# Attention by query pair first: out projection, LN1 and routing moved into the attention loop of a hybrid decoder layer

## The chip, the cores and the metric

One core of one Trainium2 chip runs the whole program. The metric is the device time of one execution, in microseconds (us). The kernel before takes 1218.9 us (median of three runs, 1218.84 to 1220.23). The profile is one further execution.

## The reference, cut to what matters

The layer takes 1024 tokens of width 1024, puts 16 meta tokens in front, and normalises them. A token mixer follows with two head groups, then one output projection, a residual and a layer norm (LN1), then a mixture of experts. Cut to what the change touches:

```python
# stick-breaking attention: 8 heads x 64, strictly causal, blocks of 128 queries
z = q @ k.T * scale
log_not_beta = where(visible, -softplus(z), 0)
between = reverse_cumsum(log_not_beta) - log_not_beta
o_sb = rms_norm(where(visible, exp(log_sigmoid(z) + between), 0) @ v, sb_norm_g)
# gated DeltaNet: 4 heads x 128, a recurrence over chunks of the sequence -> o_gdn
h = layer_norm(ALPHA * h + concat([o_sb, o_gdn]) @ w_out, ln1_g, ln1_b)    # out projection, LN1
group = top1(h @ w_group + b_group); experts = top2(expert logits in that group)   # routing
y[token] = sum over its 2 experts of SwiGLU(h[token])                     # 32 experts
out = layer_norm(ALPHA * h + y, ln2_g, ln2_b)[meta tokens dropped]
```

A query row needs all 8 heads of the attention before its out projection, and all tokens need their routing before the first expert can gather its rows, because a token's place in an expert's list is a running count over all tokens.

## The kernel before, in words

**Stages.** `phase1` normalises, projects q, k, v and the DeltaNet inputs and prepares the recurrence. `phase2` holds the attention, the recurrence, the out projection, LN1 and the routing. `phase4` runs the 32 experts and the last norm. Instructions are put in order by a planner, which walks through the program with simulated times and may start later work early where its inputs and buffers are there; attention steps have a raised priority (`high_priority`, L1332 and L1342). Inside `manual_schedule` the order is that of the program. Each engine and the DMA queue of SP then run their instructions in that order and wait where an input is missing.

**Attention.** A unit is a head h and a pair u of 128-query tiles (tiles 2u and 2u+1). It goes through four parts one loop step apart: `at_a` (L846: scores z on PE, two sigmoids on ACT, four causal masks on POOL), `at_b` (L874: two reverse scans and one product on DVE), `at_c` (L887: transposes on PE, copies on ACT) and `at_d` (L909: product with v on PE). A pair sees 416, 928, 1440 and 1952 score columns for u = 0, 1, 2, 3. `at_e` (L928) normalises the outputs that share a PSUM bank. The units (L1307) go head by head over u = 0, 1, 2 (24 units), then u = 3 for the 8 heads. For u below 3, `at_e` takes the three pairs of a head and writes them to DRAM (`mixa`, L924). `load_h` (L804) brings q and k of a head for 768 queries or for the last 256.

**What runs between.** `gseq` (L1042) is the recurrence, four parts for a tile (`g1` to `g4`); `mid1` (L1361) takes three steps of it in each of the first three loop steps, then one. `wo_load` and `wo_split` (L951, L957) bring the out projection's weights and split them in high and low parts, one of 16 pieces for each loop step, through one staging buffer. `hgen` (L1139) does the DeltaNet half of the out projection of all 8 tiles (`mix_split`, `omm`: 24 matmuls of 512 columns for a tile) and stores the sum in `hscr`. From loop step 27 `p3gen` (L1311) does the attention half of tiles 0 to 5, LN1 (`s1`), router logits (`s2`) and the choice of experts (`choose`).

**The tail.** After the loop the string `SEQ3` (L45) orders what is left: places of tiles 0 to 3 (`place`), the choices of tiles 4 and 5, the attention half, LN1 and router of tiles 6 and 7, their choices (7 alone as the last), the loads of 11 expert weight blocks of 1 MB (`load_raw`) and the splits of the first expert's weights (`split_k`, its subtractions on POOL by `SPK`). Then come `index` and the first expert's gather (`phase4`).

Of the kernel before, what the change touches and what calls it, by code (L numbers as in the profile page):

```python
# [8 lines left out]
F32 = mybir.dt.float32  # L9
# [10 lines left out]
KT = 8  # L20
# [11 lines left out]
U1 = 24  # L32
# [7 lines left out]
PX, CH_ = 6, 4  # L40
H0, HG_, GS = 10, (1, 2), (3, 1)
XB2, MH = 2, 2
RX = 1
SPH = (0, 2, 4, 6, 6, 8, 8)
SEQ3 = "A1 L4 b04 B1 L4 H5 A9 a46 L3 G3 b46 H6 p0 G9 B9 a67 p1 |0 O2 O1 H7 O9 p2 R3 b68 p5"  # L45
XN = 3
YB = 2
SPK = (0, 1, 2, 3, 4, 5, 6, 7)
SPK1 = ()
NAT = (6, 7)  # L50
HB, WS = 3, 2
PGN = (1, 1, 1, 3, 3, 3, 3, 3, 3, 3, 3)
TB2 = 2
TG, Z1 = 2, 512
Q1 = 6 * P
G2 = 3
# [10 lines left out]
LH = ((), (0, 1))  # L67
# [12 lines left out]
class Trunk:  # L80
# [39 lines left out]
    def consts(self):  # L120
# [19 lines left out]
        self.mixa = [dram.tile([Q1, n], F32, name=f"mixa{i}") for i, n in enumerate((384, 128))]  # L140
# [280 lines left out]
    def phase1b(self, es, ps):  # L421
# [192 lines left out]
        for s, (k, i) in enumerate(jobs + [("", 0)] * 2):  # L614
            for c, _ in enumerate(cv0(s, i) if k == "g" else qk(s, i) if k == "q" else range(3)):
                step[0] = s
                if s > HG:
                    for _ in range(CA if s <= 2 * HG else CB):
                        next(inv, None)
                if c == 0:  # L620
                    if s - 1 in conv:
                        cv1(conv[s - 1])
                        cv2(conv[s - 1])
            if s == 3 * HG + 3:
                self.aqk = self.stack_v.enter_context(self.pool("aqk", "left"))
                self.qk = {}
                self.load_h(0, 0, Q1)
# [176 lines left out]
    def load_h(self, h, q0, nq):  # L804
        nc = self.nc
        nk = NM + q0 + nq
        qk = self.aqk.tile([P, Q1 + 2 * (NM + Q1)], F32R, name="qk", bufs=2)
        qs, kh, kl = qk[:, :nq], qk[:, nq:nq + nk], qk[:, nq + nk:nq + 2 * nk]
        for s in range(2):
            hs = slice(s * DH, (s + 1) * DH)  # L810
            nc.sync.dma_start(qs[hs].bitcast(F32), self.qkd[h, s, 0:DH, NM + q0:NM + q0 + nq])
# [4 lines left out]
        self.qk[h, q0] = (qs, kh, kl)  # L816
        return last

    def phase2(self):
# [20 lines left out]
        qk, st, pvs = self.qk, {}, {}  # L840
# [5 lines left out]
        def at_a(h, u):  # L846
            q0 = 0 if 2 * u * P < Q1 else Q1
            qs, kh, kl = qk[h, q0]
# [5 lines left out]
            for c0 in range((N - 1) // zc * zc, -1, -zc):  # L854
                c1 = min(N, c0 + zc)
                z = ps.tile([P, zc], F32, name="z", bufs=2)
                for i in (1, 0):
                    b0 = ns[0] * i
                    q = qs[:, (2 * u + i) * P - q0:(2 * u + i + 1) * P - q0]
# [49 lines left out]
        def at_d(h, u):  # L909
            j = u if u < 3 else h % 4  # L910
# [10 lines left out]
            if u < 3 and j == 2:  # L921
                at_e(3)
                m, c = (0, h * DH) if h < 6 else (1, (h - 6) * DH)
                nc.sync.dma_start(self.mixa[m].rearrange("(t p) c -> p t c", p=P)[:, :, c:c + DH], st["mo"])  # L924
            elif j == 3:
                at_e(4, h // 4)

        def at_e(n, g=None):  # L928
            os_ = ap.tile([P, 4, P], F32, name="os")
            nc.scalar.activation(os_[:, :n], pvs[0][:, :n], AF.Copy)  # L930
            tp = ps.tile([P, 4, P], F32, name="tp", bufs=TBC[0])
            for u in range(n):
                nc.tensor.transpose(tp[:, u], os_[:, u], self.ident)
            tv = tp[:, :n].rearrange("p u (i d) -> p (u i) d", d=DH)
            sq = ap.tile([P, 4, P], F32, name="os").rearrange("p u (i d) -> p (u i) d", d=DH)[:, :2 * n]
            nc.scalar.activation(sq, tv, AF.Square)
            rs = small.tile([P, NT], F32, name="ars")[:, :2 * n]
            nc.vector.tensor_reduce(rs, sq, axis=AX, op=ALU.add)
            self.rsqrt_into(rs, rs, 1.0 / DH, RMS_EPS)
            nc.vector.tensor_tensor(sq, tv, rs[:, :, None].to_broadcast([P, 2 * n, DH]), op=ALU.mult)  # L940
            if g is None:
                nc.gpsimd.tensor_tensor(sq, sq, gs[:, None, :].to_broadcast([P, 2 * n, DH]), op=ALU.mult)
                st["mo"] = sq
                return
            for i in range(2):
                eng = nc.gpsimd if i else nc.vector
                eng.tensor_tensor(O["ms"][i][:, g * 256:(g + 1) * 256].rearrange("p (h d) -> p h d", d=DH),
                                  sq.rearrange("p (h i) d -> p h i d", i=2)[:, :, i],
                                  gs[:, None, :].to_broadcast([P, 4, DH]), op=ALU.mult)
# [18 lines left out]
        def g_load(t):  # L968
# [12 lines left out]
            c["zg"] = gp.tile([P, 512], F32, name="zg", bufs=2)  # L981
# [93 lines left out]
        def open_out():  # L1075
            op = O["op"] = os_.enter_context(self.pool("outp", "right"))
            O["ms"] = [op.tile([P, 512], F32, name=f"ms{i}") for i in range(2)]
# [42 lines left out]
        def mix_split(t, mx):  # L1120
            m = [hp.tile([P, 4, P], F32R, name=f"m{x}", bufs=MH) for x in "hl"]
            tp = ps.tile([P, 4, P], F32, name=TQ[0], bufs=TQ[1])
            for j in range(4):
                nc.tensor.transpose(tp[:, j], mx[:, j * P:(j + 1) * P], self.ident)
            self.split(tp, *m)
            T[t]["m"] = m

        def omm(t, s, k0, al):
            ht, (mh, ml) = T[t]["ht"], T[t]["m"]
            o = ps.tile([P, 4, P], F32, name=TQ[2], bufs=TQ[3]).rearrange("p a b -> p (a b)")  # L1130
            ns = slice(s * F, (s + 1) * F)
            for j in range(4):
                wh, wl = wo[k0 + j, s]
                nc.tensor.matmul(o, mh[:, j], wh, start=(j == 0), stop=False)
                nc.tensor.matmul(o, mh[:, j], wl, start=False, stop=False)
                nc.tensor.matmul(o, ml[:, j], wh, start=False, stop=(j == 3))
            nc.vector.scalar_tensor_tensor(ht[:, ns], ht[:, ns], al, o, op0=ALU.mult, op1=ALU.add)

        def hgen():  # L1139
            while gdone[0] < 1:  # L1140
                yield
            mix_load(0)
            ht_load(0)
            for t in range(NT):
                mix_split(t, T[t]["mg"])
                yield
                omm(t, 0, 4, ALPHA)
                if t + 1 < NT:
                    while gdone[0] < t + 2:
                        yield  # L1150
                    mix_load(t + 1)
                    ht_load(t + 1)
                yield
                omm(t, 1, 4, ALPHA)
                nc.sync.dma_start(self.hscr[t * P:(t + 1) * P, :], T[t]["ht"])
                yield

        def s0(t):
            ht_load(t)
            if t < 6:  # L1160
                ma = O["op"].tile([P, 512], F32, name="mxa", bufs=1)
                nc.sync.dma_start(ma[:, :384], self.mixa[0][t * P:(t + 1) * P, :])
                nc.sync.dma_start(ma[:, 384:], self.mixa[1][t * P:(t + 1) * P, :])
            else:
                ma = O["ms"][t - 6]
            yield
            mix_split(t, ma)

        def s1(t):
            c = T[t]  # L1170
            ht = c["ht"]
            for s in range(2):
                omm(t, s, 0, 1.0)
                yield
            if t < 6:
                rs = self.ln_stats(ht, P)
                self.ln_apply(ht, P, rs, ht)
                for v, w in ((O["g1"], ALU.mult), (O["b1"], ALU.add)):
                    nc.vector.tensor_tensor(ht, ht, v, op=w)
            else:  # L1180
                c["st"] = mv, rs = self.ln_stats(ht, P, raw=True)
                yield
                nc.vector.scalar_tensor_tensor(rs[:, 1:2], mv[:, 0:1], -1.0, rs[:, 0:1], op0=ALU.mult, op1=ALU.mult)
                self.ln_apply(ht, P, rs, ht)
                for v, w in ((O["g1"], ALU.mult), (O["b1"], ALU.add)):
                    for h in range(2):
                        (nc.gpsimd if h in LH[t - 6] else nc.vector).tensor_tensor(
# [643 lines left out]
```

## Time and profile before

| | before |
|---|---|
| median of 3 runs | 1218.9 us |
| the profiled execution | 1214.15 us |
| its span, first to last instruction | 1212.3 us |
| PE busy in the span | 1087.4 us (90%) |
| DVE busy | 867.2 us (72%) |
| ACT busy | 624.9 us (52%) |
| POOL busy | 375.2 us (31%) |
| DMA | 259.20 MB, mean 214 GB/s |

PE is the matrix engine (TensorE), PEld its weight loads, DVE the vector engine, ACT the scalar engine, POOL is GpSimd, SP issues most DMAs. A busy share is an average over stages; what holds a stage is read from that stage. A name like `tp<-ident,be` is output from inputs; L899 is line 899 of the kernel. The granted clock of PE is given as a share of 2.4 GHz.

### The profile page before, as it was taken

The page shows a single profiled execution, that of the slowest core. Times are in us where ns is not written, and L with a number is a line of the kernel's source. Part 1 is how long each engine was busy: PE and PEld are TensorE (multiplying, and loading weights), DVE is VectorE, ACT ScalarE, POOL GpSimd, SP SyncE. Part 2 cuts the span into 40 slices and gives each one's busy share as a digit, 9 for nine tenths or more (in the row PEclk, how much of TensorE's full clock was granted, in tenths as well). Part 3 has the DMA queues.
Part 4 walks back from the last instruction along what each step waited for, and adds up shares of the span by engine and source line. Part 5 has one row for each costly group of instructions (what it writes and reads, how often), then busy time and mean ns, then how long its engine had stood idle before and what let it go on. Part 6 is the DMA issues. An engine that isn't in the chain of part 4 may idle for free. (4 is left out here: it accounts for less than half of the span.)

```text
span 1212.3 us, 19733 instructions
## 1 busy us (share of the span) xinstructions
PE 1087.4 (90%) x7029; PEld 925.1 (76%) x7029; DVE 867.2 (72%) x1588; ACT 624.9 (52%) x1310; POOL 375.2 (31%) x423
## 2 busy tenths in 40 slices
PE   6999999999899989789999999839999899989981
PEld 4999999999899868678777778736776666666661
DVE  7941357889433258888857687877997787887978
ACT  3443346845233244555546453326776566666754
POOL 3523103502000037666624341141222122122325
PEclk9999999999999978999989999958999999999996
DMA  7411124465896478765657672957999999998353
GB/s 284 174 62 44 54 88 124 149 199 177 249 269 206 156 243 234 220 211 152 187 158 192 209 235 101 405 219 238 343 348 333 310 324 324 325 321 270 80 197 139
DMA packets 111285, 259.20 MB, mean 214 GB/s; under 512 B 32804, under 2 KB 62252, under 8 KB 98386
## 3 DMA queue, kind: packets, MB, share of 16 engines
q1 hardware_dynamic: 101680, 239.57, 58.8%
q0 software_dynamic: 9216, 17.28, 6.1%
q8 instruction: 56, 0.92, 0.3%
q10 hardware_dynamic: 290, 1.07, 0.2%
q14 instruction: 43, 0.35, 0.1%
HBM read 205.44 MB, written 68.72 MB: 226 GB/s over the span
## 5 line engine op out<-in xcount | busy, mean ns | idle before, releaser
L184 PE MATMUL pj<-hTh,wfh 128*128 128x346 f32 (+1 forms) x480 | 156.0, 325 | 0.1
L186 PE MATMUL pj<-hTh,wfl 128*128 128x346 f32 (+1 forms) x480 | 155.6, 324 | 0.0
L185 PE MATMUL pj<-hTl,wfh 128*128 128x346 f32 (+1 forms) x480 | 155.6, 324 | 0.0
L1570 POOL DMA_INDIRECT res<-y,ix x30 | 53.4, 1780 | 233.6 <-DVE y L1566 167.1
L879 DVE TENSOR_TENSOR_SCAN mm<-mm,zero 128x272 f32<-128x272 f32 (+3 forms) x64 | 96.1, 1522 | 28.7 <-ACT mm L866 26.1
L184 PEld LDWEIGHTS pj<-hTh,wfh 128*128 128x128 f32 x480 | 90.8, 189 | 0.5 <-issue 0.3
L186 PEld LDWEIGHTS pj<-hTh,wfl 128*128 128x128 f32 x480 | 90.8, 189 | 0.1
L185 PEld LDWEIGHTS pj<-hTl,wfh 128*128 128x128 f32 x480 | 90.7, 189 | 0.2
L1461 DVE TENSOR_TENSOR w13l<-raw,w13h 128x512 fp32r<-128x512 f32 x144 | 88.9, 686 | 0.0
L1529 PE MATMUL ph<-w13h,xh 128*128 128x512 f32 x192 | 88.8, 463 | 0.0
L177 PE MATMUL pj<-wvh,hTl 128*128 128x256 f32 (+3 forms) x280 | 79.1, 286 | 3.6 <-DVE hTl L95 3.6
L176 PE MATMUL pj<-wvl,hTh 128*128 128x256 f32 (+3 forms) x280 | 79.2, 285 | 2.2 <-DVE wvl L95 2.2
L175 PE MATMUL pj<-wvh,hTh 128*128 128x256 f32 (+3 forms) x280 | 79.6, 288 | 0.3 <-ACT hTh L94 0.3
L1460 ACT ACTIVATE w13h<-raw 128x512 fp32r<-128x512 f32 x144 | 77.8, 624 | 0.0
L1531 PE MATMUL ph<-w13h,xl 128*128 128x512 f32 x192 | 75.3, 392 | 0.0
L1530 PE MATMUL ph<-w13l,xh 128*128 128x512 f32 x192 | 75.2, 391 | 0.0
L866 ACT ACTIVATE mm<-z 128x512 f32<-128x512 f32 (+1 forms) x80 | 44.1, 565 | 49.3 <-PE z L864 35.0
L870 POOL TENSOR_SCALAR_AFFINE_SELECT mm<-mm 128x128 f32<-128x128 f32 x64 | 38.6, 613 | 91.9 <-ACT mm L866 91.4
L864 PE MATMUL z<-qk 128*128 128x416 f32 (+6 forms) x224 | 61.9, 382 | 5.4 <-ACT kuw L776 3.6
L94 ACT ACTIVATE xh<-tp 128x512 fp32r<-128x512 f32 x64 | 31.4, 490 | 59.4 <-DVE xf L1516 52.9
L1461 DVE TENSOR_TENSOR w2l<-raw,w2h 128x512 fp32r<-128x512 f32 x96 | 60.0, 688 | 2.1
L870 POOL TENSOR_SCALAR_AFFINE_SELECT be<-be 128x128 f32<-128x128 f32 x64 | 47.4, 750 | 27.3 <-ACT be L867 23.0
(432 smaller groups left out, 2984.7 us busy)
## 6 DMA issues: line engine op xcount, KB each, us to landing
raw<-in_w SPq DMA_DIRECT2D x72, 1024.0 KB, 19.8
qk<-qkd SPq DMA_DIRECT2D x16, 520.0 KB, 5.3
ht<-hscr SPq DMA_DIRECT2D x16, 512.0 KB, 5.2
qk<-qkd SPq DMA_DIRECT2D x16, 392.0 KB, 6.8
kqvd<-y SPq DMA_DIRECT2D x12, 520.0 KB, 2.9
wfr<-in_w_gdn SPq DMA_DIRECT2D x12, 512.0 KB, 3.5
wo4h<-in_w SPq DMA_DIRECT2D x6, 1024.0 KB, 19.8
wo4l<-in_w SPq DMA_DIRECT2D x6, 1024.0 KB, 13.7
```

The costliest lines, as they stand in the source:

```text
L175: nc.tensor.matmul(o[:p, :n], xh, wh[:, kt, ws], start=(kt == 0), stop=False)
L176: nc.tensor.matmul(o[:p, :n], xh, wl[:, kt, ws], start=False, stop=False)
L177: nc.tensor.matmul(o[:p, :n], xl, wh[:, kt, ws], start=False, stop=(kt == KT - 1))
L184: nc.tensor.matmul(o[:, :n], wh[:, kt], self.hTh[:, kt, c0:c0 + n], start=(kt == 0), stop=False)
L185: nc.tensor.matmul(o[:, :n], wh[:, kt], self.hTl[:, kt, c0:c0 + n], start=False, stop=False)
L186: nc.tensor.matmul(o[:, :n], wl[:, kt], self.hTh[:, kt, c0:c0 + n], start=False, stop=(kt == KT - 1))
L870: nc.gpsimd.affine_select(out=v[:, e - P:e], in_=v[:, e - P:e], pattern=[[-1, P]], compare_op=ALU.is_gt, fill=fill, base=0, channel_multip ...
L879: nc.vector.tensor_tensor_scan(mm[:, c0:c1][:, ::-1], mm[:, c0:c1][:, ::-1], self.zero1.to_broadcast([P, c1 - c0]), 1.0, op0=ALU.mult, op1 ...
L1460: nc.scalar.activation(wh, raw, AF.Copy)
L1461: (nc.gpsimd if k in pool else nc.vector).tensor_tensor(wl, raw, wh.bitcast(F32), op=ALU.subtract)
L1529: nc.tensor.matmul(ph, xh[:, kt], wh, start=False, stop=False)
L1531: nc.tensor.matmul(ph, xl[:, kt], wh, start=False, stop=(kt == ks[-1]))
```

## The change

The units go by pair first: all 8 heads of u = 0, then of u = 1, 2 and 3. `at_e` always takes four heads of one pair and keeps the result in SBUF (`MS`, two buffers for each tile of a pair); `mixa` is gone, and its last product moves from POOL to DVE. `load_h` loads q and k for each unit (four DMAs, 32 units instead of 16 loads). The recurrence goes two steps in each loop step from the first on; `wo_load` and `wo_split` go two pieces a step. The buffer of the recurrence's gate `zg` is one instead of two.

From loop step 14 on `hgen` takes three of its steps for each loop step, five from step 24 on. It does tiles 0 to 3 whole (both halves of the out projection in one PSUM group, LN1, router, `choose` and `place` for each pair); then the DeltaNet half of tiles 4 to 7, stored to `hscr` and loaded again; then the attention half, LN1 and routing of tiles 4 and 5 once u = 2 is done; then heads 0 to 3 for tiles 6 and 7. LN1 (`norm1`) is four fused DVE instructions of 512 columns instead of one on ACT and two of 1024 columns on DVE. The tail holds heads 4 to 7 for tiles 6 and 7 (12 matmuls a tile), their LN1, router, one `choose` and one `place` for both, all in program order; the eleven weight loads are issued first, and the first expert's splits subtract on DVE.

```diff
+PS, PN = 14, (3, 5)
...
-        units = [(h, u) for h in range(HA) for u in range(3)] + [(h, 3) for h in range(HA)]
+        units = [(h, u) for u in range(4) for h in range(HA)]
...
-            c["zg"] = gp.tile([P, 512], F32, name="zg", bufs=2)
+            c["zg"] = gp.tile([P, 512], F32, name="zg", bufs=1)
...
+        def norm1(t):
+            ht = T[t]["ht"]
+            mv, rs = T[t]["st"]
+            for h in range(2):
+                ns = slice(h * F, (h + 1) * F)
+                nc.vector.scalar_tensor_tensor(ht[:, ns], ht[:, ns], mv[:, 0:1], O["g1"][:, ns],
+                                               op0=ALU.subtract, op1=ALU.mult)
+            for h in range(2):
+                ns = slice(h * F, (h + 1) * F)
+                nc.vector.scalar_tensor_tensor(ht[:, ns], ht[:, ns], rs[:, 0:1], O["b1"][:, ns],
+                                               op0=ALU.mult, op1=ALU.add)
...
+        def ogen(t):
+            u, i = t // 2, t % 2
+            mg = mix_split([(T[t]["mg"], 0, 4)])
+            yield
+            terms = [(4 + j, mg, j) for j in range(4)]
+            if t >= 4:
+                for s in range(2):
+                    omm(t, s, terms, ALPHA)
+                    yield
+                return
+            ma = mix_split([(MS[u][i], 0, 4)])
+            yield
+            for s in range(2):
+                omm(t, s, terms + [(j, ma, j) for j in range(4)], ALPHA)
+                yield
+            yield from fin1(t)
...
         def mid(s):
-            mid1(s)
-            if s >= H0:
-                for _ in range(HG_[0] if s < U1 else HG_[1]):
-                    if next(hg, 0) == 0 and not self.raws:
-                        self.load_raw(4)
-            if "op" in O and "cg" not in O:
-                fold()
-            if s >= U1 + 3:
-                for _ in range(PGN[s - U1]):
-                    next(pg, None)
+            wo_step()
+            for _ in range(2):
+                if next(gen, 0) == 0 and "op" not in O:
+                    gs_.close()
+                    open_out()
+                    fold()
+            if s >= PS and "op" in O:
+                for _ in range(PN[s >= 3 * HA]):
+                    next(hg, None)
...
+        self.load_raw(11)
+        split(0, 1)
+        for t in (6, 7):
...
+            for s in range(2):
+                omm(t, s, [(2 + j, ma, 2 * (t - 6) + j) for j in range(2)], 1.0)
+                nc.vector.bn_stats(st[0][:, s], T[t]["ht"][:, s * F:(s + 1) * F])
+            nc.vector.bn_aggr(st[1], st[0].rearrange("p a b -> p (a b)"))
+            self.rsqrt_into(st[2][:, 0:1], st[1][:, 1:2], 1.0, LN_EPS)
+            if t == 6:
+                split(1, 2)
+            s2(t, "wg")
+            norm1(t)
+            s3(t)
+        choose(6, 8)
+        place(6, 8)
         self.index(acc[:, :NE], NE, self.ix)
```

## Rows read from the trace of the kernel before

**Rows 1.** Busy time by stage: stretch, length, busy us (instructions) of each engine, clock, DMA.
```profile
437.00:605.00 168.00, 149.02 (x1103) 123.27 (x1104) 137.61 (x180) 89.59 (x195) 109.97 (x139) 0.91 0.68 204
605.00:625.00 20.00, 18.22 (x96) 15.08 (x96) 8.10 (x10) 5.80 (x14) 4.34 (x8) 0.74 0.55 173
625.00:750.00 125.00, 121.62 (x839) 95.53 (x840) 93.49 (x124) 65.99 (x133) 43.33 (x39) 1.00 0.62 183
750.00:820.00 70.00, 44.49 (x262) 39.66 (x262) 53.61 (x212) 21.82 (x44) 19.79 (x19) 0.79 0.74 291
```
**Rows 2.** DVE groups by shape, 437 to 605 us: busy us, mean ns, idle before.
```profile
L879 DVE TENSOR_TENSOR_SCAN mm<-mm,zero 128x784 f32<-128x784 f32 x8 | 15.8, 1976 | 6.7 <-ACT mm L866 6.5 <-POOL mm L870 0.2
L882 DVE TENSOR_TENSOR be<-be,mm 128x1439 f32<-128x1439 f32 x7 | 12.1, 1733 | 0.2
L879 DVE TENSOR_TENSOR_SCAN mm<-mm,zero 128x656 f32<-128x656 f32 x7 | 12.0, 1712 | 5.4 <-ACT mm L866 5.4
L879 DVE TENSOR_TENSOR_SCAN mm<-mm,zero 128x528 f32<-128x528 f32 x8 | 11.9, 1491 | 0.7 <-POOL mm L870 0.4 <-ACT mm L866 0.3
L882 DVE TENSOR_TENSOR be<-be,mm 128x927 f32<-128x927 f32 x8 | 9.9, 1233 | 0.7 <-POOL be L870 0.4
L879 DVE TENSOR_TENSOR_SCAN mm<-mm,zero 128x400 f32<-128x400 f32 x8 | 8.9, 1118 | 0.0
L1137 DVE SCALAR_TENSOR_TENSOR ht<-ht,tg 128x512 f32<-128x512 f32 x8 | 5.4, 674 | 1.2 <-PE tg L1136 1.2
```
**Rows 3.** POOL groups by shape, 437 to 605 us.
```profile
L870 POOL TENSOR_SCALAR_AFFINE_SELECT be<-be 128x128 f32<-128x128 f32 x46 | 28.7, 638 | 11.3 <-ACT be L867 11.0
L870 POOL TENSOR_SCALAR_AFFINE_SELECT mm<-mm 128x128 f32<-128x128 f32 x48 | 22.8, 488 | 52.1 <-ACT mm L866 51.7 <-DMA wst<-in_w_out 0.3
L942 POOL TENSOR_TENSOR os<-os,gs 128x384 f32<-128x384 f32 x6 | 7.3, 1220 | 1.1 <-DVE fr L1033 0.8 <-DVE os L940 0.2
```
**Rows 4.** PE in order of time, 720 to 800 us: start, us, line.
```profile
725.55 0.74 PE L864 MATMUL z<-qk 128*128 128x512 f32 x2
726.13 1.03 PE L899 MATMUL tp<-ident,be 128*128 128x128 f32 x8
...
729.99 0.39 PE L1136 MATMUL tg<-w13h,ml 128*128 128x512 f32 x1
730.22 0.39 PE L1134 MATMUL tg<-w13h,mh 128*128 128x512 f32 x1
...
736.73 1.98 PE L1204 MATMUL tp<-wr,h1T 128*128 128x36 f32 x16
...
747.96 1.97 PE L919 MATMUL pv<-wt,vt 128*64 128x128 f32 x30
...
794.83 3.47 PE L1204 MATMUL tq<-wg,h1T 128*128 128x36 f32 x16
```
**Rows 5.** DVE in order of time in the tail.
```profile
773.01 0.16 DVE L1227 TENSOR_REDUCE fm<-lg 128x2 f32<-128x8 f32 x1
...
780.71 0.22 DVE L1271 TENSOR_TENSOR ohs<-oh 128x64 f32<-128x64 f32 x1
...
804.52 0.99 DVE L1230 SCALAR_TENSOR_TENSOR fu<-ing,fm,desc 128x8 f32<-128x8 f32 x1
...
810.03 0.28 DVE L1294 TENSOR_TENSOR px<-oh,rq 128x128 f32<-128x128 f32 x1
...
813.75 0.19 DVE L1471 SCALAR_TENSOR_TENSOR ix<-acc,ie 128x32 int32<-128x32 f32 x1
```
**Rows 6.** PE in order of time, the first expert's transposes.
```profile
820.00 1.94 PE L1507 MATMUL tp<-ident,xg 128*128 128x128 f32 x8 [6.39 <-DMA xg<-h1d,ix]
```
**Rows 7.** The DMA queue of SP in order of time.
```profile
426.19 1.37 SPq L1114 DMA_DIRECT2D ht<-hscr  x3
```
**Rows 8.** Busy time in one stretch of 5 us of the tail, columns as in group 1.
```profile
775.00:780.00 5.00, 4.66 (x24) 3.69 (x23) 4.28 (x22) 0.77 (x3) 0.00 (x0) 1.00 1.02 426
```

More of the change, by code (lines that the diff above doesn't have):

```diff
@@ L909, in at_d @@
         def at_d(h, u):
-            j = u if u < 3 else h % 4
+            j = h % 4
             if j == 0:
@@ L920, in at_d, with at_e @@
                                  start=False, stop=(kb == 2 * u + i))
[L921 to L928, printed above, removed]
+            if j == 3:
+                at_e(u, h // 4)
+        def at_e(u, g):
+            if g == 0:
+                MS[u] = [ap.tile([P, 512], F32, name=f"ms{i}", bufs=2) for i in range(2)]
@@ L929, in at_e @@
             os_ = ap.tile([P, 4, P], F32, name="os")
-            nc.scalar.activation(os_[:, :n], pvs[0][:, :n], AF.Copy)
+            nc.scalar.activation(os_, pvs[0], AF.Copy)
             tp = ps.tile([P, 4, P], F32, name="tp", bufs=TBC[0])
[L932 to L935, printed above, removed]
+            for j in range(4):
+                nc.tensor.transpose(tp[:, j], os_[:, j], self.ident)
@@ L1118, in mix_load, with mix_split @@
             nc.sync.dma_start(mg, self.mixg[t * P:(t + 1) * P, :])
-        def mix_split(t, mx):
-            m = [hp.tile([P, 4, P], F32R, name=f"m{x}", bufs=MH) for x in "hl"]
+        def mix_split(parts):
+            n = sum(j1 - j0 for _, j0, j1 in parts)
+            m = [hp.tile([P, 4, P], F32R, name=f"m{x}", bufs=MH)[:, :n] for x in "hl"]
             tp = ps.tile([P, 4, P], F32, name=TQ[0], bufs=TQ[1])
[L1123 to L1126, printed above, removed]
@@ L1128, in omm @@
-        def omm(t, s, k0, al):
-            ht, (mh, ml) = T[t]["ht"], T[t]["m"]
+            i = 0
+            for mx, j0, j1 in parts:
+                for j in range(j0, j1):
+                    nc.tensor.transpose(tp[:, i], mx[:, j * P:(j + 1) * P], self.ident)
+                    i += 1
+            self.split(tp[:, :n], *m)
+            return m
+        def omm(t, s, terms, al):
+            ht = T[t]["ht"]
             o = ps.tile([P, 4, P], F32, name=TQ[2], bufs=TQ[3]).rearrange("p a b -> p (a b)")
@@ L1158, in s0 @@
[L1158 to L1187, printed above, removed]
-                            ht[:, h * F:(h + 1) * F], ht[:, h * F:(h + 1) * F], v[:, h * F:(h + 1) * F], op=w)
@@ L1346, in att, with pre, wo_step @@
                         at_a(*units[s])
[L1348 to L1354 removed]
+        wraw, wi = [None], [-2 * WS]
+        def pre(s):
+            if s + 1 < len(units):
+                wraw[0] = load_h(*units[s + 1])
+            wo_step()
+        def wo_step():
+            i = wi[0]
+            wi[0] += 1
             if 0 < i <= 16:
@@ L1359, in pre1, with mid @@
                     wraw[1:] = [wo_load(i)]
-        def mid1(s):
-            for _ in range(GS[0] if s < G2 else GS[1]):
+        hg = hgen()
+        self.raws = {}
+        def mid(s):
+            wo_step()
+            for _ in range(2):
                 if next(gen, 0) == 0 and "op" not in O:
@@ L1430, in phase2 @@
         self.dump("nov", self.nov)
+        split(6, 8)
         os_.close()
```

206 lines of the change are left out of this document (93 added, 113 removed).

## The prediction

> **What bounds the kernel now.** I read the busy time by stage first [rows 1], because the change touches only the stretch from the first score matmul (437 us) to the first expert's transposes (820 us) [rows 6]; what lies ahead and the experts behind it I leave as they are. In the row of 437 to 605 (24 units of pairs 0 to 2, the whole recurrence, four tiles of the DeltaNet half) no engine is full: PE 149.0 of 168 us at a mean clock of 0.91, DVE 137.6, POOL 110.0. In 605 to 625 the recurrence ends and the router's folded weights are made, at a clock of 0.74. In 625 to 750 PE is the bound: 121.6 of 125 us at full clock, beside 93.5 of DVE. From 750 to 820 PE has 44.5 of 70 us; its first part is still out projection at full clock, and the rest is a chain of small DVE instructions, a router pass and a gather [rows 4 to 6]. So 383 us in all, and the question is what each microsecond moved out of the last 70 costs where it lands.
>
> **The first 14 steps after the change** hold 8 units of pair 0, 6 of pair 1 and the whole recurrence. I take the row of 437 to 605 and subtract what leaves it: 8 units of pair 2, 2 of pair 1, the out projection of four tiles, 3 or 4 `at_e`.
> DVE: pair 2 costs 15.8 + 12.1 + 12.0 = 39.9 us, a quarter of pair 1's 11.9 + 9.9 + 8.9 is 7.7, eight accumulations 5.4 and five low parts at the same price 3.4 [rows 2]; `at_e`, fewer but wider, about 2. 137.6 - 58.4 = 79 us.
> POOL: 38 fewer masks at (28.7 + 22.8) / 94 = 0.55 us are 20.8; the gain on POOL (7.3) goes to DVE, some 6 us of roots go [rows 3]. 110.0 - 34 = 76 us.
> PE, priced from start to start [rows 4]: a score column 0.29 / 512 us, a transpose 0.13, a product with v 0.066, an out projection matmul 0.23. A unit of pair 2 is 2 x 1440 columns (1.6) + 11 transposes (1.4) + 22 products (1.5) + 0.8 for the meta tokens = 5.3 us, one of pair 1 is 3.7, a tile's half 24 x 0.23 + 0.6 = 6.1. So 149.0 - 8 x 5.3 - 2 x 3.7 - 4 x 6.1 - 2 = 73 us.
> PE thus stops being what holds this stretch; DVE and POOL do, and neither thins out as PE does. Before, DVE and POOL together did (137.6 + 110.0) / 168 = 1.47 us of work in each microsecond; at that rate 79 + 76 = 155 us take 105 us. The ends: 81 us if DVE alone sets it and is as full as PE in 625 to 750 (97%), 155 us if the two never overlap. I take 105, the rate of the same instructions side by side.
> A rule bears on that upper end. What the rows show: a select on 128 columns takes 0.49 and 0.64 us on the mean here and DVE's 8-element instruction at 804.52 takes 0.99 us where the reduction of 8 at 773.01 takes 0.16 [rows 3, 5]. The Trainium skill, SBUF — State Buffer, section "SBUF: two separate sides", calls the port pair that DVE and GpSimd share "an exclusive lock", held for the whole instruction. By that rule taken for every instruction the stretch would be 155 us; the trace does not bear it out that far, since before 1.47 fits in each microsecond.
> The shorter gate buffer makes SP hold the next `zg` load until `g4` of the tile ahead is done, and what is queued behind it on SP (q and k of the next unit, weight pieces) waits as well; the planner can place it late, so I take 0 and keep up to 10 us for the range. SP issues 64 more loads of q and k, about 0.5 us each by three issues in 1.37 us [rows 7], 32 us spread over 350 in which SP has little else: 0. The second weight piece per step goes through the one staging buffer; nothing needs it before step 14: 0.
>
> **The rest of the loop.** PE's work up to 750 us is 149.0 + 18.2 + 121.6 = 288.8 us. Moved in from the tail: tile 5's attention half (6.1), half of that of tiles 6 and 7 (6.1), three routers at 1.0 + 2.0 us (9), two `place` (7, by matmuls of this size): 28 us. After the first 14 steps there remain 288.8 + 28 - 73 = 244 us of PE, and DVE has about 200: 93.5 + 8.1, the 58 that left the first stretch, and some 40 for LN1, choices and the wider `at_e`. PE stays the bound; at its share in 625 to 750 (121.6 / 125) 244 us take 251. Ends: 244 if never idle, 265 if it falls to 92% because DVE is fuller than in 625 to 750. The fused LN1 (four instructions at the 0.67 us of a 512-column one [rows 2], 2.7 us of DVE a tile) and the dropped store and reload of four tiles lie beside PE: 0.
> The planner may pull some of this into the first 14 steps, where PE is free 32 us: it did start loads early (three tile loads at 426 [rows 7], ahead of the loop, for work of step 10). A tile's product needs the last weights (step 9) and all heads of pair 0 (step 11), so only three steps, 22 us with a third of PE free, are open: 8 us, between 0 and 10.
> The loop: 105 + 251 - 8 = 348 us instead of 313. **+35 us.**
>
> **The tail** runs now from 749.9 (the last product with v [rows 4]) to 820.0: 70 us. After: `at_e` alone, seven to nine short instructions one after the other at about the 0.67 us of a 512-column one [rows 2], 6; its transposes and split 2; 12 matmuls 2.8; last accumulation, transposes, copies and router of tile 6 4.6, between the 2.0 and 3.5 that 16 router matmuls take at the two clocks [rows 4] plus 1.8; the same for tile 7, which follow in program order on PE, 2.8 + 4.6; logits 0.7; `choose` for two tiles 6.5 (7.7 from 773.01 to 780.71 with other work in it); `place` and index 3.9 (810.03 to 813.94) [rows 5]; gather 6.1 [rows 6]. Sum 40. PE has idle stretches there, and before it ran at half clock after 790 (router pass of 3.47 instead of 1.98 us [rows 4]); 24 matmuls at half clock cost 5 more: 45 (ends 38 and 50). The 11 MB in front of tiles 6 and 7's stores pass in 26 us at 426 GB/s [rows 8], ahead of the index: 0. The first expert's splits on DVE stand in the gather's wait: 0. **-25 us.** This is mostly work moved, not idle time removed: before, PE idles 25.5 us of this stretch, after it about 30.
>
> **Sum.** +35 - 25 = +10; I take +9, since a part of the low-clock stretching of 437 to 625 may go. From the profiled execution (1214.15 us: 1212.3 of span and 1.85 around it) 1223; the median is 4.75 us above that execution, so 1228 us.
>
> **Rivals.**
> *Faster: the recurrence's stage overlaps better.* If DVE and POOL, with shorter scans, reach 1.8 in each microsecond, the stage takes 155 / 1.8 = 86 us; with 10 us pulled forward and a tail of 40: 86 + 251 - 10 + 40 = 367 for 383, 1203 us. For it: DVE is idle 30 of 168 us there, much of it on sigmoids of long units [rows 2], which leave. Against: pair 0's units are short, so masks and hand-overs weigh more. It decides from 96 us on. Chance 0.30.
> *No change:* the stage takes 96 us and the rest as forecast, 1219. Chance 0.13.
> *Much slower: the two engines exclude each other (the rule above).* 155 + 251 + 45 - 8 = 443, 1279 us. Against it the 1.47. Chance 0.05.
> *Slower by a late chain:* PE below 93% in steps 14 to 30, because `choose` and `place` hold banks that the attention's transposes share: 244 / 0.92 = 265, 1242 us. For it: DVE gets some 80% full there. Chance 0.14, inside the slower side.
>
> **How the numbers follow.** The forecast with its neighbourhood has 0.38. 8 in 10 lie from 1203 to 1250: the faster rival to its centre, the late chain whole, the exclusion left out. 0.2% is 2.4 us, about what a measurement here can tell. Faster 0.30, same 0.13, slower 0.38 + 0.14 + 0.05 = 0.57; the likeliest case's own range is 1222 to 1240.
>
> **What would show it.** Right: the last recurrence product about 105 us after the first score matmul, PE some 70% full until then and DVE and POOL fuller; PE 95% or more full for the next 230 us; 45 us from the last product with v to the first expert's transposes. Wrong: a first stretch under 96 us, PE below 240 us of work behind it, or a tail under 38 us.

## The result, and the profile after

The kernel after takes 1337.6 us (median of 4 runs, 1332.3 to 1340.3), the one before beside it 1219.6: a ratio of 1.0947, 95% interval 1.0906 to 1.0987. The forecast was 1228, the range 1203 to 1250. The sign was right, the size was off by 110 us, and what made the kernel slow is not what the sum had in it, so the sign says little. The profiled execution took 1336.55 us (span 1334.7), 122.4 more than that of before.

In DVE's and POOL's groups by shape, 428 to 525 us, the lines that answer to [rows 2, 3] are no dearer (a scan of 528 took 1.49 us before, this mask 0.64), so single instructions don't explain it:

```profile
L868 DVE TENSOR_TENSOR_SCAN mm<-mm,zero 128x528 f32<-128x528 f32 x7 | 9.5, 1353 | 2.2 <-ACT mm L855 2.2
```
```profile
L859 POOL TENSOR_SCALAR_AFFINE_SELECT be<-be 128x128 f32<-128x128 f32 x30 | 14.4, 494 | 3.1 <-ACT be L856 2.8
```

The experts' part is the same: from the first expert's transposes to the end 392.6 us, before 392.3. All of the difference lies ahead of it. The lines of before map to these after: score matmul L864 to L853, mask L870 to L859, scan L879 to L868, product with v L919 to L908, transposes of the products `be` L899 to L888, out projection L1134-L1136 to L1120-L1122, `place` L1287 and L1303 to L1304 and L1320, gather's transposes L1507 to L1504.

Busy time by stage, columns as in [rows 1]; the four stretches are from the first score matmul to about the end of the first 14 steps (the scores of pairs 0 and 1 are through by then), the one around the fold of the router's weights, the rest of the loop, and the tail from the last product with v to the first expert's transposes.

```profile
428.00:525.00 97.00, 73.36 (x565) 62.23 (x563) 74.15 (x108) 45.19 (x98) 54.97 (x81) 0.89 0.92 254
525.00:581.00 56.00, 16.05 (x74) 15.28 (x75) 17.88 (x37) 6.33 (x11) 17.93 (x18) 0.56 0.40 112
581.00:893.00 312.00, 264.51 (x1567) 214.14 (x1565) 173.35 (x294) 118.16 (x244) 59.85 (x76) 0.83 0.39 110
893.00:942.00 49.00, 20.26 (x98) 16.35 (x96) 27.00 (x89) 9.81 (x18) 6.91 (x6) 0.64 0.88 354
```

In the second row no engine has a third of the time. In the third PE, at full clock and 97% in the row of 625 to 750 before [rows 1], has 85% at a mean clock of 0.83. The loop is 465 us where the forecast had 348 and before 313.

What PE waited for from 428 to 893, by line: us in all, times, longest.

```profile
PE tp L1087 <- POOL wg L1084: 32.9, 1, 32.9
PE tp L1217 <- DVE ht L1134: 21.6, 6, 5.0
...
PE tp L1304 <- DVE ohs L1288: 7.9, 2, 5.0
PE tp L1320 <- DVE ohp L1319: 7.1, 3, 4.9
PE tg L990 <- DMA kuw<-kud: 6.1, 1, 6.1
```

L1087, L1217, L1304 and L1320 make 69.5 us, and none of them was in the forecast: one long wait (for the router's folded weights), and three that recur with every tile (the router) or pair of tiles (`place`, which has two). Before, PE idles 19 us in all of 437 to 605 and 3.4 us in 625 to 750 [rows 1].

**The long wait.** PE in order of time, as in [rows 4]:

```profile
538.94 1.91 PE L1004 MATMUL tg<-v,G 128*128 128x128 f32 x8
573.73 3.63 PE L1087 MATMUL tp<-wg,ones 128*128 128x36 f32 x16 [32.88 <-POOL wg L1084]
577.17 3.61 PE L1089 MATMUL tp<-wr,gb 128*128 128x36 f32 x16
...
582.32 1.06 PE L888 MATMUL tp<-ident,be 128*128 128x128 f32 x4
```

The recurrence's last product ends at 540.9. The next instruction in PE's order is `fold` (L1087), which multiplies ones by the router weights `wg`. The attention's transposes (L888) are queued behind it, and no matmul of theirs goes ahead. (The Trainium skill, TensorE: Matmul & The Clock Gate, section "Step-by-step: what each phase is for", has matmuls stay in program order; the trace agrees, with these 32.88 us.) The kernel before made the same product at the end of its recurrence, with out projection and attention ahead of it in PE's order. Its wait there is the longest of all from 605 to 750:

```profile
PE tp L1105 <- POOL wg L1102: 1.8, 1, 1.8
```

On POOL, in SP's queue and on ACT, in order of time, one sees why `wg` is late:

```profile
544.47 1.59 POOL L1022 TENSOR_TENSOR mg<-mg,zg 128x512 f32<-128x512 f32 x1
...
555.58 1.26 POOL L1022 TENSOR_TENSOR mg<-mg,zg 128x512 f32<-128x512 f32 x1
...
564.71 1.26 POOL L1022 TENSOR_TENSOR mg<-mg,zg 128x512 f32<-128x512 f32 x1
...
573.01 0.67 POOL L1084 TENSOR_TENSOR wg<-wr,gb 128x288 f32<-128x288 f32 x1 [6.57 <-DMA gb<-in_ln_gb]
```
```profile
546.08 0.33 SPq L965 DMA_DIRECT2D zg<-zgd  x1
...
556.87 0.32 SPq L965 DMA_DIRECT2D zg<-zgd  x1
557.24 9.08 SPq L1023 DMA_DIRECT2D mixg<-mg  x2
566.37 0.42 SPq L1071 DMA_DIRECT2D g<-in_ln_g  x1
...
568.36 0.53 SPq L1078 DMA_DIRECT2D gb<-in_ln_gb  x1
```
```profile
550.19 0.63 ACT L1013 ACTIVATE mg<-o 128x512 f32<-128x512 f32 x1 [1.94 <-DMA mixg<-mg]
...
560.43 0.63 ACT L1013 ACTIVATE mg<-o 128x512 f32<-128x512 f32 x1 [8.19 <-DMA mixg<-mg]
```

`g4` (square on ACT, sum, root, two products on POOL, store) goes through one buffer `mg`: the square of the next tile (550.2, 560.4) waits until the store of the last has landed, 3.2 and 3.7 us behind its issue, and 5.5 to 6.7 us of chain follow. So one tile's `g4` follows the other by 9 to 11 us, and three of them still stand behind the recurrence's last matrix product. `open_out` takes the recurrence's memory, so SP issues LN1's gains and the router weights only behind the last store (566.4), and `wg` follows at 573.0. From its fourth loop step on the kernel before took one step of the recurrence in each, where this one takes two; what that pace has to do with the wait was not tested.

**The recurring waits**, PE in order of time:

```profile
625.95 1.04 PE L853 MATMUL z<-qk 128*128 128x416 f32 x6
631.95 1.97 PE L1217 MATMUL tp<-ident,ht 128*128 128x128 f32 x8 [4.96 <-DVE ht L1134]
...
653.06 0.66 PE L1304 MATMUL tp<-ohs,triS 128*128 128x64 f32 x2 [4.98 <-DVE ohs L1288]
```

Behind a tile's last out projection only six score matmuls stand ahead of its router (L1217), which needs LN1 from DVE: statistics, root, four products. The next transposes of a unit (L888, at 636.2) are behind it in PE's order, though DVE had finished their input at 624.4 (L871). The same holds for `place` behind `choose` (L1304 needs `ohs`, the chosen experts as ones and zeros). In the kernel before, `p3gen` wrote the router of a tile one tile later (`s2(t - 1)` behind `s1(t)`), and PE has no wait for LN1 from 605 to 750. Behind these two waits PE runs at the lower level of its clock (1.2 of 2.4 GHz; granted 0.50 from 631.9 to 647 and from 653 to 660): the eight transposes at 631.95 take 1.97 us, eight at 726.13 before took 1.03 [rows 4].

**The tail**: SP's queue, then GpSimd's gather, the index on DVE that it needs, and the first expert's transposes, which answer to [rows 6].

```profile
893.21 14.33 SPq L1445 DMA_DIRECT2D raw<-in_w  x11
...
917.85 0.32 SPq L1136 DMA_DIRECT2D h1d<-ht  x1
918.21 0.43 SPq L1137 DMA_DIRECT2D res<-ht  x1
```
```profile
933.62 1.34 POOL L1494 DMA_INDIRECT xg<-h1d,ix  x1 [17.37 <-DMA res<-ht]
```
```profile
928.37 0.19 DVE L1468 SCALAR_TENSOR_TENSOR ix<-acc,ie 128x32 int32<-128x32 f32 x1
```
```profile
942.15 1.97 PE L1504 MATMUL tp<-ident,xg 128*128 128x128 f32 x8 [13.91 <-DMA xg<-h1d,ix]
```

Index ready at 928.6, gather issued at 933.6 behind the landing of tile 7's rows: these were issued at 918 behind 11 MB of weight loads. The wait is 13.9 us where [rows 6] has 6.39. Of the 7.5 us between them 4.1 are the later issue (5.0 us behind the index, before 0.9), and 3.4 the gather itself (8.5 us from its first issue to the transposes, before 5.1).

### The profile page after: what moved, and what is told of

The parts are those of the page before. It is cut to its first block, busy times and chain, and to the rows that moved or that the text cites. A ratio compares the mean times of both kernels' runs of the same rounds, so it can differ in the third digit from the quotient of the medians.

```text
span 1334.7 us, 19739 instructions
## 1 busy us (share of the span) xinstructions
PE 1124.5 (84%) x7031; PEld 956.6 (72%) x7031; DVE 865.3 (65%) x1587; ACT 618.9 (46%) x1294; POOL 336.4 (25%) x401
## 5 line engine op out<-in xcount | busy, mean ns | idle before, releaser
L868 DVE TENSOR_TENSOR_SCAN mm<-mm,zero 128x272 f32<-128x272 f32 (+3 forms) x64 | 92.6, 1467 | 46.6 <-ACT mm L855 42.6
L855 ACT ACTIVATE mm<-z 128x416 f32<-128x416 f32 (+1 forms) x80 | 44.8, 565 | 86.4 <-PE z L853 81.6
L859 POOL TENSOR_SCALAR_AFFINE_SELECT mm<-mm 128x128 f32<-128x128 f32 x64 | 39.7, 630 | 150.1 <-ACT mm L855 150.1
L889 ACT ACTIVATE wt<-tp 128x512 f32<-128x512 f32 (+1 forms) x80 | 42.5, 558 | 71.5 <-PE tp L888 64.8
L859 POOL TENSOR_SCALAR_AFFINE_SELECT be<-be 128x128 f32<-128x128 f32 x64 | 35.6, 564 | 123.8 <-ACT be L856 115.9
L853 PE MATMUL z<-qk 128*128 128x416 f32 (+5 forms) x224 | 58.3, 370 | 10.1 <-DMA qk<-qkd 5.6
L85 ACT ACTIVATE xh<-tp 128x512 fp32r<-128x512 f32 x64 | 31.3, 489 | 68.1 <-DVE xf L1513 53.3
```

The costliest lines, as they stand in the source:

```text
L859: nc.gpsimd.affine_select(out=v[:, e - P:e], in_=v[:, e - P:e], pattern=[[-1, P]], compare_op=ALU.is_gt, fill=fill, base=0, channel_multip ...
L868: nc.vector.tensor_tensor_scan(mm[:, c0:c1][:, ::-1], mm[:, c0:c1][:, ::-1], self.zero1.to_broadcast([P, c1 - c0]), 1.0, op0=ALU.mult, op1 ...
```

## The experiments

The theory: PE takes its instructions in order, and the change puts three kinds of them (fold, router, `place` after `choose`, each waiting for another engine's chain) ahead of attention work that is ready. The rivals: DVE and POOL bound the loop as a stage, so that a moved instruction changes nothing; the loads of the first steps bound it; or the pace at which steps are taken does. All are edits of the kernel after, in single runs unless a median is given; runs of that kernel scatter by 8 us, and the kernel before takes 1221 to 1226 beside them, in one run or in the median.

**1. The fold later.**
```diff
                     open_out()
-                    fold()
+            if s == 30:
+                fold()
```


> The changed kernel with the folding of the router weights (one product on POOL, 32 small matmuls, two DVE instructions) issued in loop step 30 instead of step 14; its result is first read in the tail. Theory A: PE stands in its order at these matmuls for 32.9 us of the 56 empty us (525 to 581) while attention units that are ready wait behind them; then the stall shrinks to the rest of the recurrence's chain and the time falls by 30 to 45 us, to 1292 to 1307 us. Rival: the end of the recurrence itself holds everything, since LN1's gains lie in its memory; then PE waits at the next instruction that needs them and the time falls by less than 10 us.

Measured: 1304.3, 33 less. PE passes the fold, but now stands first at out projection and then at the router of tile 0, which needs LN1's gains from the same late memory:

```profile
547.76 0.80 PE L1120 MATMUL tg<-wo4h,mh 128*128 128x512 f32 x1 [7.00 <-DVE o L986]
575.03 1.97 PE L1217 MATMUL tp<-ident,ht 128*128 128x128 f32 x8 [13.54 <-DVE ht L1134]
```

**2. Two `zg` buffers** (and one of `v`, for the memory).
```diff
-            c["zg"] = gp.tile([P, 512], F32, name="zg", bufs=1)
+            c["zg"] = gp.tile([P, 512], F32, name="zg", bufs=2)
```


> The changed kernel with two buffers for the gate zg again (the recurrence's v gets one, whose readers are through before the next is written). Theory: with one buffer the last tiles of the recurrence go one by one, some 10 us each (gate loaded only after the tile ahead has used it), and end at 567 us; with two they take some 6 us each and PE's long wait ends 10 to 15 us earlier: 1322 to 1327 us. Rival: the single product buffer mg and the weight pieces through one staging buffer set these 10 us; then less than 3 us.

Measured: 1323.8, 14 less, over the scatter but not far over it. The fold still waits 31.3 us, `wg` comes at 567.9, only 5 us sooner: the chain through `mg` remains. The other 9 lie behind it, at a granted clock of 0.87 instead of 0.83, with the router's waits as they were (22.1 us); that they come from the buffer is not shown.

**3. Router, `choose` and `place` one tile later.**
```diff
-                elif t % 2:
-                    choose(t - 1, t + 1)
+                if 1 <= t <= 4:
+                    route(t - 1)
                     yield
-                    place(t - 1, t + 1)
+                if t in (2, 4):
+                    choose(t - 2, t)
+                    yield
+                    place(t - 2, t)
                     yield
...
+            for t in (4, 5):
+                route(t)
+                yield
```


> The changed kernel with router, choice and place of each tile issued one tile later, behind the next tile's out projection (for tiles 4 and 5: both routers behind both LN1s). Theory B: from 581 to 878 PE loses its time by standing in order at router transposes that wait for LN1 on DVE (21.6 us in six waits) and at half clock after each; then 25 to 45 us less, 1292 to 1312 us. Rival: PE is thin there because attention delivers too slowly; then less than 10 us.

Measured: 1297.2, 40 less. The router's waits are gone, that of the fold stays, and those of `place` grow from 15.0 to 21.9 us:

```profile
PE tp L1087 <- POOL wg L1084: 34.3, 1, 34.3
PE tp L1311 <- DVE ohs L1295: 15.2, 3, 7.9
...
PE tp L1327 <- DVE ohp L1326: 6.7, 3, 4.5
```

Waits of 21.6 us gave 40. From 581 to the last product with v the idle time of PE fell by only 13 us (47.5 to 34.8) and its busy time by 28 (264.5 to 236.2), at a granted clock of 0.91 instead of 0.83.

**4. `place` alone one tile later.**
```diff
-                    place(t - 1, t + 1)
+                if t in (2, 4):
+                    place(t - 2, t)
```


> The changed kernel with place of tiles 0, 1 and of 2, 3 issued one tile's out projection later than choose. Theory B, second part: PE stands about 5 us at place's first matmul behind the chain of choose on DVE, and at half clock around it; two of three such waits go: 10 to 20 us less, 1317 to 1327 us. Rival: those waits only take the place of others; less than 5 us.

Measured: 1327.3, 10 less, about the scatter of the runs. The waits at `place`'s first matmul (7.9 us) are gone, and those of the router grew from 21.6 to 26.6 us.

**5. The four edits together** (with `place(4, 6)` behind the products of tiles 6 and 7).

> All four edits on the changed kernel: folding late, two gate buffers, router and choice one tile later, place one tile after that (that of tiles 4 and 5 behind the product of tiles 6 and 7). Theory: the four waits stand at different places and are PE's own, so what the single edits gave adds up: 33 + 14 + 40 + 10 = 97 us less, 1240 us, still some 20 us over the kernel before, which is the price of the order by pair itself (steps without enough PE work first, then PE full). Rival: the waits share a common releaser and only part adds, 1260 us or more; other rival: without the stalls the shorter tail shows and it falls under 1219 us.

Measured: 1235.8; measured again (run 14), a median of 1234.2. The parts add to 33 + 14 + 40 + 10 = 97 us, together they give 103; each part is a single run, so the two agree within the scatter. Its stages, columns as above:

```profile
428.00:525.00 97.00, 77.70 (x591) 66.46 (x592) 76.31 (x119) 46.58 (x101) 58.34 (x85) 0.88 0.97 267
525.00:581.00 56.00, 49.85 (x302) 38.99 (x301) 43.72 (x64) 23.61 (x48) 28.78 (x32) 0.94 0.63 177
581.00:786.00 205.00, 187.79 (x1304) 150.85 (x1302) 142.05 (x255) 95.70 (x203) 50.77 (x59) 0.96 0.52 143
786.00:835.00 49.00, 20.03 (x97) 16.43 (x98) 26.92 (x89) 9.52 (x18) 6.91 (x6) 0.63 0.89 355
```

The loop, counted from 428, is 358 us instead of 465. Of the 107, idle time of PE is 465 - 353.9 = 111 less 358 - 315.3 = 43, so 68; the other 39 are the same instructions in fewer busy microseconds (353.9 and 315.3), at a granted clock of 0.94 and 0.96 in the second and third row instead of 0.56 and 0.83. DVE has 262 us in the loop and POOL 138, after the change 265 and 133: the work is the same, so it did not bound the loop at 465 us, and that rival falls for these 107. For the first 97 us, in which the two do about as much as before the edits, this settles nothing.

**6. The square written over `u`** (as 5, to free `mg` for the next tile).
```diff
-            sq = gp.tile([P, HG, P], F32, name="mg", bufs=1)
+            sq = c["u"]
```


> The same with the squares of the recurrence's last part written over its u, which is dead by then, instead of into the one buffer mg. Theory: the end of the recurrence waits on that buffer (the squares of a tile wait for the store of the tile before, 8.2 us at the longest); 8 to 15 us less than the run with four edits. Rival: the weight pieces through one staging buffer hold ACT there; less than 3 us.

Measured: 1243.5, 7.6 more than run 5, in one run, where kernel 5 ranges from 1231.6 to 1242.5 (run 14): no gain. The buffer `mg` did hold the end of the recurrence: the last product of `g4` on POOL (L1022) starts at 538.6 instead of 560.9, and `wg` comes at 548.7 instead of 569.5. With the fold out of the way it ends sooner for nothing: PE now waits 9.8 us for the products `be` of DVE, in run 5 1.0.

**7. The first stretch alone**: edits 1, 2 and 6, no later router.

> Folding late, two gate buffers and the squares over u, and nothing of the router's edits: the first stage alone. Theory: 33 + 14 + about 10 less than the changed kernel, 1280 us, and PE's waits for LN1 and place in the loop stay as they were (about 35 us of idle). Rival: with the first stage mended the loop's waits shrink too, since attention is ahead; 1265 us or less.

Measured: 1303.8, as edit 1 alone, 24 over the expectation. The router's waits (21.3 us) are untouched by it, and PE then waits 14.3 us for the split weights of the out projection, which here are not ready when the recurrence's memory is.

**8. The tail's stores ahead of seven of the loads.**
```diff
-        self.load_raw(11)
+        self.load_raw(4)
...
+        self.load_raw(7)
         choose(6, 8)
```


> The changed kernel with one edit in its tail: 4 of the 11 raw weight loads are issued there at once, the other 7 only behind the stores of h1 rows and residual rows of tiles 6 and 7. Theory (the first expert's gather starts late because the rows of tile 7 are stored behind 11 MB of loads): the wait of the first expert's transposes for the gather falls from 13.9 to 6 to 7 us, the tail from 49 to 41 to 43 us, and the time from about 1336 to 1327 to 1331. Rival (the gather is late by itself, or its reads then lie among the 7 loads instead): the wait stays over 12 us and the time within 3 us of 1336. The experts' part stays at 355 us by either; if it grows, the later loads were needed there.

Measured: 1334.0, no difference within the scatter. (The experts' part is 392.8 us, as it was; the 355 us of the expectation is the experts' part of no run.) In the trace the gather starts at once behind the index, and the tail is 45.4 us instead of 49:

```profile
930.33 1.58 POOL L1495 DMA_INDIRECT xg<-h1d,ix  x1 [13.24 <-DVE w13l L1459]
```

The transposes still wait 10.3 us, not 6 to 7: the gather takes 9.1 us from its first issue, beside the later loads (DMA share 1.01 from 930 to 939). Half of the theory holds.

**9. Five edits: 5 and 8.**

> The kernel of the four edits together (fold of the LN1 gains at unit step 30, two zg buffers, router and choose one tile later, place one tile later still: 1235.8) with the tail edit as well. If the edits add up: 1235.8 less 6 to 8 is 1228 to 1230, the time that the sum of the prediction came to, with the tail at 41 to 42 us instead of 48 and the loop unchanged at 359. Rival (gather's reads collide with the later loads): 1235 again.

Measured: 1237.5; the tail is 45.0 us, the loop 10 longer than in 5, counted from 428 in both (7 from each one's first score matmul).

**10, 11, 12. Other paces of that kernel**, `PN` = (2, 5), (4, 5) and (3, 6) instead of (3, 5), in this order.

> As the kernel with the four edits and the tail edit, but the steps of out projection and routing that each unit step takes are 2 instead of 3 up to step 23 (5 behind it, as before). Theory (with the in-order waits gone the loop is a sum of TensorE work, and no pace changes it): within 4 us of that kernel. Rival (the pace still decides: DVE is late for TensorE because of too many routing steps in units 14 to 23): 5 to 12 us faster, down to about 1220, with the waits for the one-hot tiles of place gone. Against: more steps left behind the last unit would lengthen the tail, 5 to 15 us slower.

> The kernel of the four edits and the tail edit (1233.3 median, 11 above the kernel before), but each unit step from 14 to 23 takes 4 steps of out projection and routing instead of 3. Pace 2 had made it 12 us longer, with more of the tiles' work left behind the last unit. If the order of steps is what is left over the sum, pace 4 gives 5 to 12 us back (1222 to 1228). If DVE is late for TensorE again at this pace, the waits for LN1 and the one-hot tiles of place grow and it is 5 to 20 us longer. If neither, it stays within 4 us, and the rest lies in the first 97 us and the tail.

> As the kernel of the four edits and the tail edit, but 6 instead of 5 steps for each unit step from 24 on: by the first theory 0 to 5 us shorter, because less stays behind the last unit; by the second (DVE late) 3 to 10 us longer.

Measured: 1249.7 (one run), 1251.3 and 1238.5 (medians of two). As ratios to the kernel before beside them they are 1.022, 1.021 and 1.011, where the pace of (3, 5) has 1.006 (run 15). None is faster, so none of these paces gives the rest back; but the first expectation, that pace changes nothing, was wrong: with 2 and with 4 it is 16 and 18 us longer than the median of run 15, mostly in more busy time of PE from 581 to the last product with v (208 and 206 us against 194 in run 15), at a clock of 0.90 and 0.89 against 0.92. The waits for `place` at L1328 did not grow at pace 4 (5.6 us in both). What sets that clock was not tested.

**13. No weight loads in the first steps** (as 5; 15 of 16 pieces are not loaded, all splits read the first, so out projection and routing use wrong weights).
```diff
+            if i:
+                return wraw[1]
             raw = hp.tile([P, 512], F32, name="wst", bufs=1)
```


> The kernel of the four edits, but 15 of the 16 loads of out projection weight pieces (256 KB each) are left out, and all 16 splits read the first piece: out projection computes with wrong weights. All other work stays. Theory (the rest over the sum is the first 14 unit steps on the DMA engines, whose share there is 97%, with 13.7 us of TensorE waits for loads of keys and of the recurrence's operands; the prediction had the second weight piece per step at 0): the first 97 us shorten by 6 to 12 us, the DMA share falls under 0.9, and the time falls from 1235.8 to 1224 to 1230. Rival (VectorE and GpSimd bound that stretch as predicted, and the full DMA share is packets that wait for nobody): within 3 us of 1235.8.

Measured: 1284.7, but other weights route other tokens: behind the gather it takes 440 us instead of 399, so only the part ahead counts. There the first expert's transposes come at 842.96, in 5 at 834.82, and both begin their scores at 426: no gain. The first stretch, to be read against that of 5:

```profile
428.00:525.00 97.00, 78.22 (x583) 65.50 (x584) 79.06 (x121) 49.52 (x108) 57.93 (x84) 0.88 0.87 242
```

The DMA share falls from 0.97 to 0.87, the work of PE, DVE and POOL in 97 us stays within 4%. The theory that the weight pieces are the rest falls. The loads of keys and of the recurrence's operands were left in, and PE still waits 2.8 and 6.2 us for them (7.5 and 6.2 in run 5), so of these loads the run says nothing.

**14, 15. Kernels 5 and 9 again, for their intervals.**

> The kernel of the four edits again, to have its interval: 1233 to 1240 by the single run, 1% slower than before (ratio 1.009 to 1.016). If the sum's terms hold, it stays over the kernel before; a ratio of 1.00 would mean that the single run had been unlucky.

> The kernel with the tail edit as well, again, to have its interval. Its single run had the tail 4 us shorter than the kernel of four edits and the loop 10 us longer, at a granted clock of 0.76 in 725 to 775 against 0.97. If that clock is chance, the median is 3 to 5 us below the kernel of four edits; if it belongs to the program, the median stays at 1236 to 1239 and the same stretch shows 0.76 again.

Measured: 1234.2 (4 runs, ratio to before 1.0103, interval 1.0037 to 1.0169) and 1233.3 (8 runs, 1.0064, 1.0030 to 1.0099): both slower than before by a per cent or less, the two not told apart. In the traced executions the five-edit kernel's tail is 44.9 us instead of 49.1, and its loop 362.7 instead of 358.9, each from its first score matmul: the gain in the tail is lost in the loop, where its clock falls again (last section). That this belongs to the program is not certain: six of its eight runs took 1232.0 to 1234.6 us, two 1224.5 and 1224.9, and these were not traced. No version tried beats the kernel before.

## Why the prediction was wrong

*The rest of the loop* is the step that failed: "PE stays the bound; at its share in 625 to 750 (121.6 / 125) 244 us take 251." The work was sized well: 73 + 244 = 317 us of PE were forecast for the loop, kernel 5 has 315. What failed is the share: behind the first 97 us PE is busy 281 of 368 us in the kernel after (76%), and 238 of 261 (91%) in kernel 5, not 97%. A share read from a stage in whose order attention and the next tile's out projection stood between a tile's out projection and its router does not carry to one in which each router follows its product almost directly. The change writes `s2` right behind `norm1` and `place` right behind `choose`; the waits of 21.6, 7.9 and 7.1 us could have been priced from the DVE chains behind them. Of these the prediction let LN1 "lie beside PE: 0" and had the choices only in DVE's sum. Such a chain is not beside PE if PE's next instruction needs its end.

*The first 14 steps.* The fold's work is in the 18.2 us of 605 to 625, but a wait for its inputs is in none of the sum's terms. Its new place, straight behind the end of the recurrence, made the largest single wait, 32.9 us; moving it gave 33. The `zg` buffer, "0 and keep up to 10 us", was 14 in one run, of which 5 are traced to it. The rate of DVE and POOL that the step used holds roughly: the last recurrence product ends 113 us behind the first score matmul (forecast 105), and DVE and POOL do (74.2 + 55.0) / 97 = 1.33 us of work in each microsecond, 1.39 in kernel 5, against 1.47. The Trainium skill, SBUF — State Buffer, section "SBUF: two separate sides", has GpSimd and certain DVE operations exclude each other on their shared port pair; taken for every instruction the sum of the two could not exceed 1.00, and the trace's 1.33 does, as before. So the rival at 1279 was not what happened. The second weight piece at 0 holds in kernel 5, where run 13 took most of the pieces' loads away and gained nothing; it failed in run 7, where PE waited 14.3 us for the split weights. The 64 loads at 0 are not shown: in the first 97 us PE waited 5.6 us for q and k in the kernel after and 7.5 in run 5, and no run left these loads out.

*Pulled forward, 8 us.* It did not come: the kernel after has no out projection before 583. What came instead, by luck, is an earlier start: the first score matmul is at 427.9 instead of 437, and no term of the sum had a reason for that.

*The tail*, 45 forecast, is 49. "Ahead of the index: 0" failed for the 11 MB: the gather's wait is 7.5 us longer, and with seven of the loads behind the stores (run 8) 3.6 of them came back. Of the 24 matmuls that the sum put at half clock only 12 were: those of tile 6 start 0.43 us apart, those of tile 7 0.23. Against that `choose` for both tiles takes 4.6 us (918.37 to 922.95), not 6.5.

*The rivals.* "Slower by a late chain" had the place (`choose` and `place`) but not the mechanism, banks of PSUM, nor the size: 21 us, where waits and the lower clock beside them made 107. The priced mechanism was not tested by itself. With the waits taken away the forecast is nearly met: kernel 5 has a median of 1234 for 1228. Its profiled execution, 1235.8 for the sum's 1223, has a loop 10 us longer than forecast, a tail 4 and an experts' part 7 longer (3 in its other traced execution, with the same code), and starts 9 earlier: 12 of 13. So the sum of the moved work, 393 us for loop and tail, was 14 short of 407, and 1234 lies so near to 1228 because of the earlier start. What holds the loop's last 10 us is open. Even then the change cost 0.6 to 1.0%.

*The signs of being wrong.* None of the three came (a first stretch under 96 us, PE below 240 us of work behind it, a tail under 38: 97, 281 and 49). All three looked for a kernel faster than forecast.

What of the clock is cause and what effect was not separated: no run kept the waits and raised the clock.

## What to carry to other kernels

Before taking a busy share from one stage to another, write down the new order of the bottleneck engine and ask of each instruction which engine's chain it ends; one that follows its own producer is a wait, however idle the producer is. Ask too what the old order put between the two: the kernel before had its router one tile later, and the change took that away. Setup work placed behind a buffer release (here the fold behind the recurrence's memory) inherits the slowest chain that holds this buffer, stores included. Such a wait may cost more than its length: here 68 us less idle time of PE came with 107 us less time, the other 39 with a higher granted clock; that the waits lowered the clock is not shown.

## What was not expected of the hardware

The lower level of the clock can hold while PE is fully busy. Windows, columns as in [rows 1], of the five-edit kernel of run 15 and then of the four-edit kernel of run 14, whose code differs only in the tail:

```profile
725.00:735.00 10.00, 9.76 (x84) 7.86 (x83) 5.14 (x3) 7.12 (x16) 3.20 (x4) 1.00 0.78 222
735.00:745.00 10.00, 7.68 (x46) 5.99 (x47) 8.85 (x23) 4.87 (x13) 2.65 (x3) 0.66 0.57 120
...
755.00:765.00 10.00, 10.00 (x39) 7.69 (x40) 4.85 (x5) 2.77 (x5) 2.62 (x2) 0.50 0.00 0
```
```profile
725.00:735.00 10.00, 9.50 (x86) 8.02 (x84) 6.01 (x11) 6.28 (x13) 1.58 (x3) 1.00 0.72 203
735.00:745.00 10.00, 7.66 (x54) 6.01 (x53) 8.59 (x16) 6.83 (x16) 3.22 (x4) 1.00 0.80 221
...
755.00:765.00 10.00, 8.98 (x65) 6.92 (x66) 7.33 (x11) 3.78 (x7) 3.96 (x5) 1.00 0.01 2
```

In both PE is nearly full from 725 to 735 and has 7.7 of 10 us from 735 to 745. In one the granted clock stays at 1.00 (2.4 GHz), in the other it falls and is 0.50 (1.2 GHz) in a window in which PE never idles. PE's instructions around the fall are the same and in the same order, 6 us apart: one behind 1.7 us of idle time, six behind another 0.67, and soon after these 30 products with v, in run 15 and then in run 14:

```profile
736.65 0.39 PE L893 MATMUL tp<-ident,be 128*16 128x128 f32 x2 [1.69 <-DVE lg L1163]
...
740.57 3.68 PE L908 MATMUL pv<-wt,vt 128*64 128x128 f32 x30
```
```profile
742.86 0.39 PE L893 MATMUL tp<-ident,be 128*16 128x128 f32 x2 [1.68 <-DVE lg L1163]
...
745.52 1.97 PE L908 MATMUL pv<-wt,vt 128*64 128x128 f32 x30
```

Both executions of the five-edit kernel that were traced show 0.76 over 725 to 775, those of the four-edit kernel 0.97 and 1.00. Why is open.
